# Four of eight pairs by seven products in the two feed-forwards, five and six of twenty-two in the first one's second product, and TensorE's order tied to the source

## The chip, the cores and the metric

The kernel runs on one core of a Trainium2 chip. The metric is the device time of one execution in microseconds. A core has five engines with a queue each, which run side by side and wait for one another by semaphores: TensorE (PE, matrix products; its weight loads, PEld, overlap the products), VectorE (DVE), ScalarE (ACT), GpSimd (POOL) and SyncE (SP). DMA transfers are issued from the queues of SP, ScalarE and GpSimd, and run on 16 DMA engines.

## The reference

One encoder layer on 256 tokens of width 2048, everything in float32: a feed-forward, a token mixer, a cross-attention into 256 memory tokens, and a second feed-forward, each behind an RMS norm and added to its input, with a last norm at the end. The change touches the two feed-forwards (hidden width 5632):

```python
def swiglu_ffn(h, w_in, w_out):
    gate, up = jnp.split(h @ w_in, 2, axis=-1)
    return (jax.nn.silu(gate) * up) @ w_out

h = rms_norm(x, ffn1_norm[l])
x = x + MACARON_SCALE * swiglu_ffn(h, ffn1_w_in[l], ffn1_w_out[l])
...
h = rms_norm(x, ffn2_norm[l])
x = x + MACARON_SCALE * swiglu_ffn(h, ffn2_w_in[l], ffn2_w_out[l])
```

## The kernel before, in words

**Products in parts.** Both sides of a float32 product are split into a high part (a cast to the type fp32r) and a low part, the remainder, and three matmuls are summed for a product: high by high, high by low, low by high (`three`, L316 to 320, and `by_two`, L322 to 334). A weight tile has 128 rows (one k) and 1024 columns. `raw` (L403 to 409) issues its load from SP into one of several raw buffers, and `parts` (L392 to 401) splits it: ScalarE casts the high part (L397), VectorE subtracts for the remainder (L398). The split buffers are used in rotation: three called hl, two called ring, and in the first feed-forward one called more from its second group on.

**Groups.** The first product of a feed-forward (by `w_in`) runs over 11 groups (`NG`) of 512 hidden features, 512 gate and 512 up columns, so a weight tile is 128x1024. A group has 16 tiles, taken as 8 pairs of neighbours. Group 0 is plain. In groups 1 to 10 (`group`, L527) the letters of a pattern (L37) say how each pair is done:

- C (`eight`, L492): two plain tiles, 12 matmuls of 128x128 by 128x512 each, into the four banks "2", "3", "4", "8".
- S (`seven`, L464): the pair is seen as a product of 2x2 blocks and done with seven block products in place of eight, as in Winograd's form of Strassen's method, so 21 matmuls in place of 24. Its seven products go into banks "5", "7", "6", "1", "2", "3", "4". It needs four split weight tiles, and I call them by their names in the code: the sums (1024 wide, formed by VectorE at L470 and 471 from the two raw tiles), "one" (1024; its left half updated at L477), "two" (1024, as loaded) and a half tile (512; "two" updated at L484). The sums serve products 5 and 7, "one" serves 6 and 1, "two" serves 2 and 3, the half tile serves 4. The four matching forms of x are made once, by `sides` (L435), beside group 0.

After the last S pair of a group `joins_sevens` (L520) puts its own four banks together: a copy of bank "1" by ScalarE (L521) and four VectorE adds (L522 to 525), which read the four `spare` slices p1, u2, u4, u5. After the last pair come the end adds (L550), one each for the banks "2", "4", "3", "8", and `give` (L507): two silus on ScalarE (L510), two multiplies on VectorE (L512). The buffer `spare` also holds the sums, some of the raw tiles and the raw tiles of the summed ones.

**Summed tiles.** A few plain tiles of a group, listed in `SUMMED` (L39), are not split by VectorE. `summed` (L419) loads them from SP (L425), ScalarE writes the negated high part (L426) and then the high part (L427), and a DMA that accumulates, issued from GpSimd (L428), adds the raw tile to the negated part. They have two buffers, hl_s and, in the first feed-forward, half of more. In the second feed-forward, groups 8 to 10 have one such buffer and the list `ALONE` (L40).

**The second product.** In the first feed-forward, the second product (by `w_out`, 44 tiles of 128x1024 for each of two output blocks in use here, that is 22 pairs a block) is done by `out_block` (L553) with the same `seven` and `eight`; `OUT_S` (L44) lists the S pairs and `OUT_STEPS` (L45) the order. Their x-side forms come out of `out_sides` (L580), behind the transposes of the hidden features (`turning`, L300, and `turn`, L656). The second product of the second feed-forward is done by `gemm_n` (L192) and not touched.

**What orders the work.** The program is built through a tile scheduler that simulates the engines' timelines and sets the order of each engine's queue from that. Work that the source lists later can so come earlier in a queue, matmuls of different pairs too. `tc.issue_after(ins)` adds an edge: what is issued inside it on the engine of `ins` stands behind `ins` in that engine's queue.

Of the kernel before, what the change touches and what calls it, by code (L numbers as in the profile page):

```python
# [11 lines left out]
F32 = mybir.dt.float32  # L12
# [32 lines left out]
OUT_STEPS = (  # L45
    [0, 1, 2, 3, 4, 5, 6, 7, 8, 10, 11, 9, 13, 14, 12, 16, 17, 15, 18, 19, 20, 21],
    [9, 0, 1, 12, 2, 3, 15, 4, 5, 18, 6, 7, 8, 10, 11, 13, 14, 16, 17, 19, 20, 21],
# [31 lines left out]
def layer(ctx: ExitStack, tc: tile.TileContext, a: dict):  # L79
# [220 lines left out]
    def turning(o, c, sink):  # L300

        def go():
            tp = pa.tile([P, 2, T], F32, name="aux")
            for k in range(2):
                for t in range(2):
                    nc.tensor.transpose(  # L306
                        out=tp[:, k, t * P:(t + 1) * P], in_=o[:, t, c + k * P:c + (k + 1) * P], identity=ident
                    )
            sink(tp)
        return go  # L310
# [5 lines left out]
    def three(acc, x, hi, lo, first, last):  # L316
# [3 lines left out]
        nc.tensor.matmul(acc, lhsT=x[1], rhs=hi, start=False, stop=last)  # L320

    def by_two(acc, x, hi, lo, k, first, last):  # L322
# [5 lines left out]
        for t in range(2):  # L328
# [4 lines left out]
            for g in range(2):  # L333
                nc.tensor.matmul(acc[t][g], lhsT=x[:, 1, s], rhs=hi[:, cols[g]], start=False, stop=last)  # L334
# [7 lines left out]
    class FeedForward:  # L342
# [6 lines left out]
        def __init__(self, stack, tags, x_hl, gain, w_in, pattern, summed, w_out=None, pair=False):  # L349
# [34 lines left out]
            self.next = None  # L384
# [34 lines left out]
        def summed(self, at):  # L419
# [5 lines left out]
            nc.sync.dma_start(out=raw, in_=self.w_in[j, :, k])  # L425
# [32 lines left out]

        def begins(self, name):
# [4 lines left out]
        def seven(self, j, p, b, last):  # L464

            k = 2 * p
# [19 lines left out]
            three(b["4"], self.half(j, k + 1, 1), w[:, 0, lo], w[:, 1, lo], self.begins("4"), False)  # L486
# [5 lines left out]
        def eight(self, j, p, b, last, plain, between=None):  # L492
            for k in (2 * p, 2 * p + 1):
# [7 lines left out]
                by_two(acc, self.x(j, k), w[:, 0], w[:, 1], k, begin, last and k % 2 == 1)  # L501
# [18 lines left out]
        def joins_sevens(self, b, p1, u2, u4, u5):  # L520
# [4 lines left out]
            nc.vector.tensor_tensor(out=u5, in0=u2, in1=b["5"], op=ALU.add)  # L525

        def group(self, j, r, after=()):  # L527
# [8 lines left out]
            n = len(self.pattern)  # L536
            for p, c in enumerate(self.pattern):
                if c == "S":
                    self.seven(j, p, b, p == self.spairs[-1])
                    if p == self.spairs[-1]:  # L540
                        self.joins_sevens(b, p1, u2, u4, u5)
                else:
                    late = p > self.spairs[-1] and len(after) > 0
                    self.eight(j, p, b, p == n - 1, late)
                    if p > self.spairs[-1] + 1:
# [110 lines left out]
        def turn(self, i):  # L656

            def go():
# [17 lines left out]
                turning(self.h[i // 2], i % 2 * 2 * P, both)()  # L676
# [13 lines left out]
    with ExitStack() as stack:  # L690
# [7 lines left out]
        def x_more(k):  # L698
# [4 lines left out]
            if k in (6, 9, 12):  # L703
                ff.sides(k // 3 - 2)
# [665 lines left out]
```

## Time and profile before

| what | value |
|---|---|
| three runs | 2089.42, 2089.99, 2090.06 us |
| their median | 2089.99 us |
| the profiled execution | 2088.91 us, its span 2087.1 us |
| mean granted TensorE clock | 0.999 |
| TensorE busy | 2076.4 us, 99% |
| VectorE busy | 1622.5 us, 78% |
| ScalarE busy | 1174.4 us, 56% |
| GpSimd busy | 66.0 us, 3% |

The span goes from the first to the last instruction; the time of the execution holds 1.8 us more. In the lines of the profile, each row names a line of the code, the engine, the operation, what is written and read, the shape, and then, by the view, counts, busy time and the mean of one. PE, PEld, DVE, ACT, POOL and SP are the engines; a name with q behind it is an engine's queue where it issues DMAs. A timeline's row begins with the start in microseconds from the span's start and the time until the last one of the row is through; `x3` at its end says that three instructions stand together, and brackets hold the idle time before the row and what ended it. A window's row has the stretch, its length, the busy time and the number of instructions of PE, PEld, DVE, ACT and POOL, the granted TensorE clock, the DMA engines' busy share and GB/s. Instruction times are those of one execution.

### The profile page before, as it was taken

The page shows a single profiled execution, that of the slowest core. Times are in us where ns is not written, and L with a number is a line of the kernel's source. Part 1 is how long each engine was busy: PE and PEld are TensorE (multiplying, and loading weights), DVE is VectorE, ACT ScalarE, POOL GpSimd, SP SyncE. Part 2 cuts the span into 40 slices and gives each one's busy share as a digit, 9 for nine tenths or more (in the row PEclk, how much of TensorE's full clock was granted, in tenths as well). Part 3 has the DMA queues.
Part 4 walks back from the last instruction along what each step waited for, and adds up shares of the span by engine and source line. Part 5 has one row for each costly group of instructions (what it writes and reads, how often), then busy time and mean ns, then how long its engine had stood idle before and what let it go on. Part 6 is the DMA issues. An engine that isn't in the chain of part 4 may idle for free.

```text
span 2087.1 us, 26730 instructions
## 1 busy us (share of the span) xinstructions
PE 2076.4 (99%) x9765; PEld 1739.0 (83%) x9765; DVE 1622.5 (78%) x2302; ACT 1174.4 (56%) x1470; POOL 66.0 (3%) x81
## 2 busy tenths in 40 slices
PE   9999999999999999999999999999999999999998
PEld 8888888888888888888888899888888888888886
DVE  7888888877777689989877666778888888787754
ACT  8665666555545554445764455566665655554443
POOL 0000000000000000000000000000000000000000
PEclk9999999999999999999999999999999999999999
DMA  9787778755566576655555543687777777556664
GB/s 366 246 263 246 232 223 263 230 182 192 188 203 234 180 238 199 186 179 187 180 196 192 184 160 124 200 291 224 237 236 253 222 217 230 169 166 203 195 192 152
DMA packets 122245, 441.30 MB, mean 211 GB/s; under 512 B 13569, under 2 KB 13953, under 8 KB 121729
## 3 DMA queue, kind: packets, MB, share of 16 engines
q1 hardware_dynamic: 113184, 407.08, 57.1%
q0 software_dynamic: 8352, 31.46, 8.1%
q8 instruction: 76, 1.25, 0.2%
q10 hardware_dynamic: 576, 1.06, 0.1%
q14 instruction: 57, 0.46, 0.1%
HBM read 437.44 MB, written 2.10 MB: 211 GB/s over the span
## 4 chain that ended last, share of the span: by engine, by line
PE 87%; issue 11%; POOL 1%; DMA 1%; ACT 0%; DVE 0%; DVEq 0%; POOLq 0%
PE acc L332 11%; PE acc L331 11%; PE acc L334 11%; PE acc L204 8%; PE acc L205 8%; PE acc L203 8%; PE acc L154 8%; PE acc L162 4%; PE acc L318 3%; PE acc L319 3%; PE acc L320 3%; PE aux L306 1%; PE aux L318 1%; PE aux L319 1%; PE aux L320 1%
## 5 line engine op out<-in xcount | busy, mean ns | idle before, releaser
L124 ACT CAST hl<-raw 128x1024 fp32r<-128x1024 f32 (+1 forms) x315 | 327.1, 1040 | 358.9 <-PE acc L205 191.9
L125 DVE TENSOR_TENSOR hl<-raw,hl 128x1024 fp32r<-128x1024 f32 (+1 forms) x315 | 381.2, 1212 | 165.0 <-ACT hl L124 163.6
L397 ACT CAST hl<-raw 128x1024 fp32r<-128x1024 f32 (+1 forms) x151 | 147.6, 988 | 117.3 <-PE acc L334 48.2
L398 DVE TENSOR_TENSOR hl<-raw,hl 128x1024 fp32r<-128x1024 f32 (+1 forms) x151 | 172.2, 1145 | 47.4 <-ACT hl L397 45.7
L398 DVE TENSOR_TENSOR hl<-spare,hl 128x1024 fp32r<-128x1024 f32 (+1 forms) x125 | 144.7, 1162 | 32.5 <-ACT hl L397 30.3
L397 ACT CAST hl<-spare 128x1024 fp32r<-128x1024 f32 (+1 forms) x125 | 124.3, 1002 | 66.4 <-PE acc L334 24.2
L332 PE MATMUL acc<-hl,x_hl 128*128 128x512 f32 x388 | 140.9, 390 | 0.1
L331 PE MATMUL acc<-hl,x_hl 128*128 128x512 f32 x388 | 135.7, 390 | 0.0
L334 PE MATMUL acc<-hl,x_hl 128*128 128x512 f32 x388 | 120.6, 390 | 0.0
L397 ACT CAST ring<-spare 128x1024 fp32r<-128x1024 f32 (+1 forms) x83 | 82.1, 993 | 59.6 <-issue 19.1
L398 DVE TENSOR_TENSOR ring<-spare,ring 128x1024 fp32r<-128x1024 f32 (+1 forms) x83 | 95.2, 1150 | 20.3 <-ACT ring L397 19.6
L332 PE MATMUL acc<-ring,x_hl 128*128 128x512 f32 x276 | 101.3, 389 | 0.0
L204 PE MATMUL acc<-hl,x_hl 128*128 128x512 f32 x256 | 100.7, 393 | 0.0
L204 PE MATMUL acc<-hl,m_hl 128*128 128x512 f32 x256 | 100.4, 392 | 0.0
L205 PE MATMUL acc<-hl,m_hl 128*128 128x512 f32 x256 | 100.3, 392 | 0.0
L205 PE MATMUL acc<-hl,x_hl 128*128 128x512 f32 x256 | 100.0, 391 | 0.0
L331 PE MATMUL acc<-ring,x_hl 128*128 128x512 f32 x276 | 98.6, 390 | 0.0
L203 PE MATMUL acc<-hl,m_hl 128*128 128x512 f32 x256 | 90.9, 392 | 0.0
L203 PE MATMUL acc<-hl,x_hl 128*128 128x512 f32 x256 | 90.2, 392 | 0.0
L334 PE MATMUL acc<-ring,x_hl 128*128 128x512 f32 x276 | 86.2, 389 | 0.0
L332 PEld LDWEIGHTS acc<-hl,x_hl 128*128 128x128 f32 x388 | 72.6, 188 | 15.5 <-DVE hl L133 0.4
L334 PEld LDWEIGHTS acc<-hl,x_hl 128*128 128x128 f32 x388 | 72.9, 188 | 15.1
(518 smaller groups left out, 5100.8 us busy)
## 6 DMA issues: line engine op xcount, KB each, us to landing
spare<-in_ffn_w_in SPq DMA_DIRECT2D x184, 512.0 KB, 6.8
raw<-in_ffn_w_in SPq DMA_DIRECT2D x157, 512.0 KB, 5.9
raw<-in_ffn_w_out SPq DMA_DIRECT2D x138, 512.0 KB, 4.0
hl_s<-in_ffn_w_in POOLq DMA_DIRECT2D x42, 512.0 KB, 8.3
raw<-in_w_mix_vg SPq DMA_DIRECT2D x32, 512.0 KB, 4.3
raw<-in_w_k SPq DMA_DIRECT2D x32, 512.0 KB, 3.6
raw<-in_w_v SPq DMA_DIRECT2D x32, 512.0 KB, 4.0
raw<-in_w_mix_out SPq DMA_DIRECT2D x32, 512.0 KB, 4.4
```

The source lines that it names most:

```text
L124: nc.scalar.copy(out=hl[:, 0, :size], in_=raw[:, :size])
L125: newest[0] = nc.vector.tensor_tensor(out=hl[:, 1, :size], in0=raw[:, :size], in1=hl[:, 0, :size].bitcast(F32), op=ALU.subtract)
L154: done = nc.tensor.matmul(acc, lhsT=hi[:, k], rhs=xs[k], start=first and k == 0, stop=last and k == kk - 1, skip_group_check=True,)
L162: done = nc.tensor.matmul(acc[:, 0], lhsT=lo[:, k], rhs=xs[k][:, 0], start=False, stop=last and k == kk - 1, skip_group_check=True,)
L203: nc.tensor.matmul(acc[t], lhsT=x[:, 0, s], rhs=hi[:, k], start=k0 + k == 0, stop=False)
L204: nc.tensor.matmul(acc[t], lhsT=x[:, 0, s], rhs=lo[:, k], start=False, stop=False)
L205: nc.tensor.matmul(acc[t], lhsT=x[:, 1, s], rhs=hi[:, k], start=False, stop=k0 + k == nk - 1)
L331: nc.tensor.matmul(acc[t][g], lhsT=x[:, 0, s], rhs=hi[:, cols[g]], start=(t, g) in first, stop=False)
L332: nc.tensor.matmul(acc[t][g], lhsT=x[:, 0, s], rhs=lo[:, cols[g]], start=False, stop=False)
L334: nc.tensor.matmul(acc[t][g], lhsT=x[:, 1, s], rhs=hi[:, cols[g]], start=False, stop=last)
L397: self.cast = nc.scalar.copy(out=hl[:, 0, :n], in_=raw[:, :n])
L398: newest[0] = nc.vector.tensor_tensor(out=hl[:, 1, :n], in0=raw[:, :n], in1=hl[:, 0, :n].bitcast(F32), op=ALU.subtract)
```

## The change

The pattern of a group has four S pairs in place of three, at pairs 0, 2, 4, 6, and so the last S pair is the last but one. Group 10 of both feed-forwards and groups 8 to 10 of the second keep the old pattern (`FEWER`), so 9 groups of the first and 7 of the second change. The summed tiles are k = 2, 6, 10, 14 in place of 2, 7, 13. The second product of the first feed-forward has 5 and 6 S pairs in its two blocks in place of 3 and 4, with S and C alternating in the first block from the step at which they begin, and in the second from its start; the buffers are parted otherwise for the two more forms. The summed tiles' raw loads are issued by GpSimd.

Two kinds of ties are new. `tied` holds TensorE's order to the source: each S pair, each plain tile and each pair of transposes is issued behind the last matmul of the one before. And an S pair's VectorE work (the sums, updates and remainders of `seven`) is issued behind `joined`, the last of the four joins of the group (or block) before.

The core of the diff (with the longer tables left out):

```diff
-PATTERNS = ("SCSCSCCC", "SCSCSCCC")
-SUMMED = ((2, 7, 13), (2, 7, 13))
+PATTERNS = ("SCSCSCSC", "SCSCSCSC")
+FEWER = "SCSCSCCC"
+SUMMED = ((2, 6, 10, 14), (2, 6, 10, 14))
+SIDES = (4, 7, 10, 13)
-OUT_S = ((9, 12, 15), (9, 12, 15, 18))
+OUT_S = ((9, 11, 13, 15, 17), (9, 11, 13, 15, 17, 19))
...
             j, k = self.sums_at[at]
-            nc.sync.dma_start(out=raw, in_=self.w_in[j, :, k])
+            nc.gpsimd.dma_start(out=raw, in_=self.w_in[j, :, k])
...
+        def tied(self):
+            return nullcontext() if self.pe is None else tc.issue_after(self.pe.ins)
...
         def seven(self, j, p, b, last):
+            with self.tied(), nullcontext() if self.joined is None else tc.issue_after(self.joined.ins):
+                self.seven_products(j, p, b, last)
+
+        def seven_products(self, j, p, b, last):
             k = 2 * p
...
-            three(b["4"], self.half(j, k + 1, 1), w[:, 0, lo], w[:, 1, lo], self.begins("4"), False)
+            self.pe = three(b["4"], self.half(j, k + 1, 1), w[:, 0, lo], w[:, 1, lo], self.begins("4"), False)
...
-                by_two(acc, self.x(j, k), w[:, 0], w[:, 1], k, begin, last and k % 2 == 1)
+                with self.tied():
+                    self.pe = by_two(acc, self.x(j, k), w[:, 0], w[:, 1], k, begin, last and k % 2 == 1)
...
-            nc.vector.tensor_tensor(out=u5, in0=u2, in1=b["5"], op=ALU.add)
+            self.joined = nc.vector.tensor_tensor(out=u5, in0=u2, in1=b["5"], op=ALU.add)
...
-            n = len(self.pattern)
-            for p, c in enumerate(self.pattern):
+            pattern = FEWER if j == NG - 1 or self.pair and j > 7 else self.pattern
+            n, done = len(pattern), pattern.rindex("S")
+            for p, c in enumerate(pattern):
...
-            self.sums_at = [(j, k) for j in range(1, NG) for k in sums if j < NG - 1 or k < min(14, sums[-1])]
+            self.sums_at = [(j, k) for j in range(1, NG) for k in sums if j < NG - 1 or k < 13]
...
-                turning(self.h[i // 2], i % 2 * 2 * P, both)()
+                with self.tied():
+                    self.pe = turning(self.h[i // 2], i % 2 * 2 * P, both)()
...
-                ff.ring += [more[:, q] for q in range(2)]
-                forms = more[:, 2:].rearrange("p a two n -> p (a two n)")
+                ff.ring.append(more[:, 0])
+                forms = more[:, 1:].rearrange("p a two n -> p (a two n)")
...
-                rest["raws"] = [pool.tile([P, 1024], F32, name=f"raw_out{q}") for q in range(2)]
+                ff.ring.append(pool.tile([P, 2, 1024], F32R, name="hl_out"))
...
-        ff.raws = rest["raws"]
-        xT = xt.tile([P, KD, T], F32, name="xT", tag="x")
-        for k in range(0, KD, 8):
-            nc.gpsimd.dma_start(out=xT[:, k:k + 8], in_=a["xT"][:, k:k + 8])
...
         def beside_second(i):
             if i == OUT_STEPS[1].index(OUT_S[1][-1]):
-                ff.ring = []
+                ff.raws, ff.ring = [], ff.ring[1:]
+                xT = xt.tile([P, KD, T], F32, name="xT", tag="x")
...
-            elif i > 9:
+            elif i > 10:
                 beside(1.4)
-                if i % 2 == 0 and turns:
+                if i > 12 and i % 2 == 0 and turns:
...
-            if k in (6, 9, 12):
-                ff.sides(k // 3 - 2)
+            if k in SIDES:
+                ff.sides(SIDES.index(k))
```

VectorE at the boundary from group 5 to group 6 of the first feed-forward, in the program before. L398 are remainders; by their targets and by what stands around them, ring<-spare (first) is that of the next pair's sums, ring<-spare (second) that of "one", more<-spare that of "two", and hl<-spare of 512 that of the half tile, all of group 6's first pair; L484 updates "two" for that half tile. L470, 471 and 477 belong to its second S pair. L524 and L525 are the last two joins of group 5, L550 its first end add.

```order
L398 TENSOR_TENSOR ring_131<-spare_132,ring_131 128x1024
L524 TENSOR_TENSOR spare_132<-spare_132,aux_1680 128x512
L398 TENSOR_TENSOR ring_131<-spare_132,ring_131 128x1024
L470 TENSOR_TENSOR spare_132<-raw_2052 128x512
L471 TENSOR_TENSOR spare_132<-raw_2054,raw_2052 128x512
L525 TENSOR_TENSOR spare_132<-spare_132,acc_1679 128x512
L398 TENSOR_TENSOR more_490<-spare_132,more_490 128x1024
L477 TENSOR_TENSOR raw_2052<-spare_132,raw_2054 128x512
L484 TENSOR_TENSOR spare_132<-spare_132 128x512
L398 TENSOR_TENSOR hl_2014<-spare_132,hl_2014 128x512
L550 TENSOR_TENSOR spare_132<-spare_132,acc_1683 128x512
```

The whole first pair of group 6 stands ahead of group 5's first end add, and the sums of it ahead of the third join. In the program after, the same engine from the last join (L541) on; here L485 and 486 form the sums of group 6's first pair, ring<-raw is the remainder of "two" (raw_2021), L492 the update of "one", L567 the four end adds, L499 the update of "two", hl<-spare the remainder of the sums, hl<-raw that of tile 3 (a plain tile of pair 1) and ring<-spare that of "one".

```order
L541 TENSOR_TENSOR spare_132<-spare_132,acc_1709 128x512
L485 TENSOR_TENSOR spare_132<-spare_132 128x512
L486 TENSOR_TENSOR spare_132<-raw_2021,spare_132 128x512
L404 TENSOR_TENSOR ring_131<-raw_2021,ring_131 128x1024
L492 TENSOR_TENSOR spare_132<-spare_132,raw_2021 128x512
L567 TENSOR_TENSOR spare_132<-spare_132,acc_1713 128x512
L567 TENSOR_TENSOR spare_132<-spare_132,acc_1714 128x512
L499 TENSOR_TENSOR raw_2021<-raw_2021,spare_132 128x512
L567 TENSOR_TENSOR spare_132<-spare_132,acc_1715 128x512
L404 TENSOR_TENSOR hl_2025<-spare_132,hl_2025 128x1024
L567 TENSOR_TENSOR spare_132<-spare_132,acc_1716 128x512
L404 TENSOR_TENSOR hl_2071<-raw_2069,hl_2071 128x1024
```

All of the pair's work now stands behind the last join and lies mixed with the end adds; the remainder of "one" comes behind the last of them, and that of the half tile is further back. ScalarE at the same boundary before: L521 is the joins' copy, L397 are casts (ring twice: the sums and "one"; more: "two"; hl of 512: the half tile; the last one: tile 3), L426 and 427 the negated copy and the cast of a summed tile.

```order
L521 COPY spare_132<-acc_1682 128x512
L397 CAST hl_1932<-raw_1930 128x1024
L397 CAST hl_1953<-raw_1951 128x1024
L397 CAST ring_131<-spare_132 128x1024 x2
L397 CAST more_490<-spare_132 128x1024
L397 CAST hl_2014<-spare_132 128x512
L426 ACTIVATE hl_s_133<-spare_132 128x1024
L427 CAST hl_s_133<-spare_132 128x1024
L397 CAST hl_2033<-spare_132 128x1024
```

The casts of the pair stand ahead of the summed tile's negated copy. After, L537 is the joins' copy, ring<-raw_2021 the cast of "two", L432 and 433 the negated copy and the cast of a summed tile into the buffer that tile k = 14 leaves, hl<-spare the cast of the sums, hl<-raw that of tile 3, ring<-spare that of "one", L526 a silu.

```order
L537 COPY spare_132<-acc_1712 128x512
L403 CAST ring_131<-raw_2021 128x1024
L432 ACTIVATE more_498<-spare_132 128x1024
L433 CAST more_498<-spare_132 128x1024
L403 CAST hl_2025<-spare_132 128x1024
L403 CAST hl_2071<-raw_2069 128x1024
L403 CAST ring_131<-spare_132 128x1024
L526 ACTIVATE h5_125<-spare_132,r_x2_109 128x512
```

The casts of the sums and of "one" now stand behind the negated copy, and "two" alone ahead of it. In both programs TensorE's matmuls of the pair follow behind group 5's last tile; after, in the source's order.

More of the change, by code (lines that the diff above doesn't have):

```diff
@@ L1 @@
 from collections import deque
[L2 removed]
+from contextlib import ExitStack, nullcontext
 import numpy as np
@@ L309, in go @@
             sink(tp)
+            return done
         return go
@@ L319, in three @@
         nc.tensor.matmul(acc, lhsT=x[0], rhs=lo, start=False, stop=False)
-        nc.tensor.matmul(acc, lhsT=x[1], rhs=hi, start=False, stop=last)
+        return nc.tensor.matmul(acc, lhsT=x[1], rhs=hi, start=False, stop=last)
     def by_two(acc, x, hi, lo, k, first, last):
@@ L333, in by_two @@
             for g in range(2):
-                nc.tensor.matmul(acc[t][g], lhsT=x[:, 1, s], rhs=hi[:, cols[g]], start=False, stop=last)
+                done = nc.tensor.matmul(acc[t][g], lhsT=x[:, 1, s], rhs=hi[:, cols[g]], start=False, stop=last)
+        return done
     def bank(pool, name):
```

26 lines of the change are left out of this document (14 added, 12 removed).

## The prediction

> **What bounds the kernel now.** I read the page first, then the list of waits of TensorE, then windows of one group's length, and last the timelines of three engines around one group boundary. The page and the list of waits:
>
> ```profile
> span 2087.1 us, 26730 instructions
> PE 2076.4 (99%) x9765; PEld 1739.0 (83%) x9765; DVE 1622.5 (78%) x2302; ACT 1174.4 (56%) x1470; POOL 66.0 (3%) x81
> PE aux L232 <- DVE ones L229: 1.1, 1, 1.1
> PE acc L332 <- DMA hl_s<-in_ffn_w_in: 0.8, 1, 0.8
> ```
>
> TensorE is busy for 99% of the span and waits 1.9 us in all. So the kernel lasts as long as its matmuls take at the rate at which TensorE issues them, and no other engine costs anything as long as it keeps TensorE fed. What I need of an average group is the issue rate and the room of the others (columns: PE, PEld, DVE, ACT, POOL busy with instructions, granted clock, DMA share, GB/s):
>
> ```profile
> 213.90:255.38 41.48, 41.48 (x184) 34.36 (x184) 34.41 (x41) 26.03 (x29) 2.60 (x3) 1.00 0.78 243
> ```
>
> This is one group. Its code has 3 pairs of 21 matmuls and 5 of 24, that is 183 (the cut counts one more), so a matmul goes out every 41.48 / 183 = 0.2267 us. VectorE has 7.1 us to spare in it, ScalarE 15.4 us.
>
> Now the boundary between two groups, as it stands before (into group 8, first feed-forward). TensorE starts the next group at 339.75; I call that moment E, and times below are relative to it.
>
> ```profile
> 333.63 0.39 PE L332 MATMUL acc<-hl_s,x_hl 128*128 128x512 f32 x1
> ...
> 337.94 0.62 PE L334 MATMUL acc<-ring,x_hl 128*128 128x512 f32 x2
> ...
> 339.30 0.62 PE L334 MATMUL acc<-ring,x_hl 128*128 128x512 f32 x2
> 339.75 0.39 PE L318 MATMUL acc<-more,ring 128*128 128x512 f32 x1
> ```
>
> ```profile
> 319.84 1.03 ACT L427 CAST more<-spare 128x1024 fp32r<-128x1024 f32 x1
> 320.78 1.04 ACT L397 CAST hl<-spare 128x1024 fp32r<-128x1024 f32 x1
> 321.72 0.58 ACT L521 COPY spare<-acc 128x512 f32<-128x512 f32 x1
> ...
> 334.06 1.06 ACT L426 ACTIVATE hl_s<-spare 128x1024 fp32r<-128x1024 f32 x1 [2.85 <-PE acc L332]
> 335.03 1.04 ACT L427 CAST hl_s<-spare 128x1024 fp32r<-128x1024 f32 x1
> 336.23 0.62 ACT L397 CAST hl<-raw 128x512 fp32r<-128x512 f32 x1 [0.17 <-DVE raw L484]
> ...
> 342.32 0.72 ACT L510 ACTIVATE h<-spare,r_x 128x512 f32<-128x512 f32 x1
> 343.00 1.05 ACT L397 CAST hl<-spare 128x1024 fp32r<-128x1024 f32 x1
> ```
>
> ```profile
> 338.37 0.69 DVE L550 TENSOR_TENSOR spare<-spare,acc 128x512 f32<-128x512 f32 x1 [0.79 <-PE acc L334]
> 338.97 1.22 DVE L398 TENSOR_TENSOR ring<-spare,ring 128x1024 fp32r<-128x1024 f32 x1
> 340.11 1.88 DVE L550 TENSOR_TENSOR spare<-spare,acc 128x512 f32<-128x512 f32 x3
> 341.90 0.75 DVE L512 SCALAR_TENSOR_TENSOR h<-spare,r_x,h 128x512 f32<-128x512 f32 x1
> 342.56 1.22 DVE L398 TENSOR_TENSOR ring<-spare,ring 128x1024 fp32r<-128x1024 f32 x1
> ```
>
> Three things are to be seen. First, the prices in a full queue, start to start: VectorE 0.60 us for 128x512, 1.14 for 128x1024, 0.66 for a give; its results are there 0.69, 1.22 and 0.75 after the start. ScalarE 0.97 for the negated copy of a summed tile, 0.94 for a 1024-wide cast (done after 1.05), 0.48 for the join's copy (done after 0.58), 0.68 for a silu, 0.62 until a 512-wide cast is done. Second, both queues stop for TensorE: ScalarE's negated copy starts at 334.06, 0.04 us after the matmul of 333.63 is through (0.39 long), and VectorE idles 0.79 us before the first end add. Third, this costs nothing here, because all four weight tiles of the next group's first pair stand ahead of the end adds in VectorE's queue, and ahead of that negated copy or just behind it in ScalarE's.
>
> **The change, part by part.** The gain is plain. Of 16 groups one pair more goes from 24 to 21 matmuls, and 4 pairs more of the 44: 20 x 3 = 60 matmuls, which the built programs confirm (9726 before, 9666 after). 60 x 0.2267 = 13.6 us, if TensorE stays fed.
>
> VectorE's load can still be carried. A group gains 8 of its operations (5 x 0.60 + 3 x 1.14 = 6.4 us) and loses three remainders (3.4 us), since now four of eight ordinary tiles are summed ones: 34.4 + 3.0 = 37.4 us of 40.8. Inside a group, S and C pairs alternate: 10.2 us of TensorE against 6.4 + 1.1 us of VectorE. I followed the queues through one group of each kind and found every weight tile ready before its product. In the second product (S with two plain tiles, 8.7 us of VectorE in 10.2) each remainder also stands ahead of whatever waits for TensorE. I cost all this at nothing; the cover is five or more split buffers, two pairs of work.
>
> At the group's end the cover is gone. Two edits do it. The last S pair is now pair 6, not pair 4, so the joins can start only one C pair before the end; and the next group's S pair is tied behind the last join, so none of its VectorE work can go earlier. On top, the summed tile k = 14 lies in that last C pair, and ScalarE's negated copy into its buffer waits for it.
>
> Take the boundary into group 6, whose queues are shown with the change. Slots of 0.2267 us run back from E: pair 6 takes slots -45 to -25, tile 14 -24 to -13, tile 15 -12 to -1. ScalarE: the copy of product 1 waits for slot -34 (through at -7.32) and is done at -6.70. The negated copy waits for tile 14's tenth matmul (slot -15, through at -3.01) and starts at -2.97, its cast at -2.00, then the cast of the sums at -1.06 (done -0.01), of tile 3 at -0.12, of "one" at 0.82 (done 1.87), a silu at 1.76, the half cast at 2.44 (done 3.06). VectorE: joins at -6.66, -6.06, -5.46, -4.86; sums at -4.26 and -3.66; remainder of "two" -3.06; update of "one" -1.92; the first end add, whose gate (slot -8) opened at -1.42, at -1.32; the next at -0.72, update of "two" -0.12, third end add 0.48, remainder of the sums 1.08 (done 2.30), fourth end add 2.22, tile 3 at 2.82, remainder of "one" 3.96 (done 5.18), give 5.10, half remainder 5.76 (done 6.45).
>
> TensorE, in its own order: first products of 5 and 7 at 0.03 and 0.26; those of 6 and 1 wait for the cast of "one" and go at 1.91; all of 2 and 3 follow at 2.37 and 3.05, the first of 4 at 3.73, the rest of 5 and 7 at 3.95; the rest of 6 and 1 waits for its remainder until 5.22, the rest of 4 until 6.49. The pair ends at 6.95 instead of 21 x 0.2267 = 4.76: 2.2 us lost.
>
> There are five kinds of boundary; each is worked the same way from its queues. Into groups 3, 6, 9 of the first feed-forward: 2.2. Into 4, 7, 10 tile 3 stands behind the pair, "one" is cast at -0.12 and its remainder done at 4.04, the half remainder at 5.31: the pair ends at 5.80, 1.0 lost. Into 2, 5, 8 the update of "two" comes last of all: remainder of the sums 0.59, "one" 2.33, "two" 3.47, then two sums of the following pair and two gives, the update at 7.13, the half cast done at 8.48, one more update and remainder, the half remainder at 9.47 (done 10.16). TensorE waits from 5.6 to 8.5 and from 8.8 to 10.2 and ends at 10.65: 5.9 lost. Into 2 to 7 of the last feed-forward: half remainder done at 6.45 as above, 2.2 each; into 8, where no negated copy stands in the way but two sums do, 3.4. The shortened groups behind have the old order, 0. Sum: 3 x (2.2 + 1.0 + 5.9) + 6 x 2.2 + 3.4 = 27.3 + 16.6 = 43.9 us.
>
> The trace of before has no such stall, so I bound it. The nearest row from below is the 0.8 us in the list of waits; from above, a VectorE that does nothing of the pair ahead of time, 6.4 us of its work. What I take lies between, at the queue's own prices. Elsewhere: loads for summed tiles move from SP to POOL, ahead of the accumulating DMA.
>
> ```profile
> hl_s<-in_ffn_w_in POOLq DMA_DIRECT2D x42, 512.0 KB, 8.3
> 0.74 0.86 SPq L603 DMA_DIRECT2D raw<-in_ffn_w_in  x2
> 5.37 0.47 PE L331 MATMUL acc<-hl,x_hl 128*128 128x512 f32 x1
> 3.20:4.50 1.30, 1.30 (x8) 1.30 (x8) 0.00 (x0) 0.58 (x2) 0.00 (x0) 1.00 1.07 383
> ```
>
> An accumulation lands 8.3 us after its issue and has over 15 us until its tile is used, so it stays hidden. SP loses a queue's worth of waits that cost nothing. But POOL's first load now waits for nothing and goes out beside the first weights, with the DMA engines full: 524 KB at 383 GB/s is 1.4 us ahead of the first matmul, or nothing if it comes second. I take 0.7.
>
> Sum against the profiled execution (2088.91): -13.6 + 43.9 + 0.7 = +31.0, 2119.9. The median of the three runs is 1.1 us higher, so 2121 us.
>
> **Rivals.** (1) The queues run ahead as before and the matmuls saved are all that counts: 2089.99 - 13.6 + 0.7 = 2077 us, faster. For it: VectorE keeps 3 us to spare per group, and the trace has no wait at any boundary. Against: the order after. It decides at a stall of 13.6 / 16 = 0.85 us per boundary. 5%.
>
> (2) Only ScalarE's gate counts, VectorE being earlier than I think: 1.5, 0.5, 1.0 and 0.5 us by kind, 12 us in all, 2089 us: the same. 3%.
>
> (3) TensorE slows down after the long stalls. The rows that bear on it:
>
> ```profile
> 1.10:3.20 2.10, 2.10 (x10) 2.10 (x11) 0.00 (x0) 1.49 (x3) 0.21 (x1) 1.00 0.62 160
> 717.94 0.93 PE L306 MATMUL aux<-ident,o 128*128 128x128 f32 x7
> 2075.00:2087.00 12.00, 3.35 (x15) 2.44 (x13) 5.05 (x14) 4.31 (x10) 2.56 (x2) 0.86 0.45 175
> ```
>
> Coming from idle, the first 128-wide matmuls stand 0.21 us apart, those at 718 us (0.93 - 0.27) / 6 = 0.11; and the granted clock falls to 0.86 in the tail, where TensorE has run dry. If a stall of the longest kind (one matmul between 5.6 and 10.2) did the same, the 21 or so matmuls behind it would take 4.8 us more, in three places: +14 us, 2135. Against it: shorter idle times leave the clock at 1.00. 13%. [...]
>
> (4) The accumulating DMAs come late, now that two DMAs a tile share POOL's queue and DMA is at 0.82: at 2 us a group, 32 us more, 2153. Against: 15 us of cover. 7%.
>
> **The numbers.** The forecast has 72%. Its own errors are the stall's prices, 30% low (2107) to 15% high (2128). The range 2106 to 2142 takes in rival 3 and leaves out rivals 1, 2 and 4, 15%. A measurement here tells 0.2% (4 us) from no change: faster 0.05, same 0.03, slower 0.92.
>
> **What would show it.** In the profile after, the groups should show 180 matmuls in some 42 to 47 us instead of 41.5; TensorE's list of waits should name ScalarE's casts and VectorE's remainders of the split tiles with about 44 us, all at group ends, none in the second product. If waits are under 15 us, I am wrong; if they lie inside the groups, the mechanism is another; if the clock falls below 1.00 at the boundaries, it is rival 3.

## The result and the profile after

The changed kernel takes 2144.66 us (median of four runs, 2143.42 to 2145.36) against 2090.02 us: slower, ratio 1.0263, 95% interval 1.025 to 1.0275. That is 54.6 us more, where the forecast was 31 and its range ended at 2142. The profiled execution took 2145.36 us, 56.4 more than the one of before.

The page after, its span and the engines' busy time, and the largest entries of TensorE's list of waits:

```profile
span 2143.6 us, 26789 instructions
PE 2096.7 (98%) x9705; PEld 1728.2 (81%) x9705; DVE 1691.4 (79%) x2427; ACT 1221.3 (57%) x1539; POOL 121.2 (6%) x171
...
PE acc L324 <- DVE ring L404: 13.2, 12, 2.4
PE acc L323 <- ACT ring L403: 7.8, 3, 2.6
PE acc L324 <- DVE more_out L404: 2.2, 1, 2.2
```

TensorE has 60 matmuls fewer and yet 20 us more busy time: 13.6 us of work went, so some 34 us of "busy" came in without a matmul more. In the rows below matmuls stand 0.427 us apart at a granted clock of 0.50, in place of 0.2267, and single ones beside a wait count 0.39 and 0.49 us of busy time. The waits are the ones the prediction named (L324 waits for a remainder, L323 for a cast), and there is an entry in the second product (more_out) that it did not. The prediction looked for about 44 us in this list, all at group ends; the entries for casts, remainders and end adds in the groups add up to some 32, those of the second product to 3.0, and the rest of the loss stands in TensorE's busy time.

Four groups, each from its first matmul to the next group's first (columns as in the windows before). The first three are groups 5, 6 and 7 of the first feed-forward, the last is group 4 of the second one. A group now has 180 matmuls, 180 x 0.2267 = 40.8 us:

```profile
227.44:277.09 49.65, 45.17 (x181) 35.20 (x180) 37.47 (x47) 28.00 (x32) 5.70 (x8) 0.93 0.73 210
277.09:321.06 43.97, 42.18 (x182) 33.40 (x181) 37.10 (x47) 27.95 (x32) 5.67 (x8) 1.00 0.81 239
321.06:363.40 42.34, 41.82 (x182) 33.48 (x181) 36.86 (x47) 27.80 (x32) 5.70 (x8) 1.00 0.86 251
1537.23:1580.73 43.50, 42.09 (x182) 33.41 (x181) 37.21 (x47) 28.04 (x32) 5.69 (x8) 1.00 0.81 242
```

They lose 8.8, 3.2, 1.5 and 2.7 us, where the hand-made queues gave 5.9, 2.2, 1.0 and 2.2: the kinds of boundary are right, the period of three too. Nearly all of it lies in the first two pairs of the group; groups 3, 6 and 9 lose 0.4 to 0.5 us more in their third S pair. VectorE's 36.9 to 37.5 us a group are as forecast (37.4). The first row alone has a granted clock below 1.00.

Inside that row, TensorE around the longest wait, and four windows of 3.41 us from it on:

```profile
233.19 0.39 PE L325 MATMUL acc<-hl,ring 128*128 128x512 f32 x1
236.17 0.49 PE L323 MATMUL acc<-ring,x_hl 128*128 128x512 f32 x1 [2.59 <-ACT ring L403]
237.86 0.80 PE L324 MATMUL acc<-ring,x_hl 128*128 128x512 f32 x1 [1.20 <-DVE ring L404]
238.45 0.63 PE L325 MATMUL acc<-ring,x_hl 128*128 128x512 f32 x1
238.88 0.63 PE L336 MATMUL acc<-hl_s,x_hl 128*128 128x512 f32 x1
```

```profile
233.13:236.54 3.41, 0.82 (x3) 0.20 (x2) 3.41 (x6) 1.97 (x3) 0.00 (x0) 1.00 0.03 5
236.54:239.95 3.41, 2.21 (x6) 1.71 (x6) 3.41 (x5) 2.52 (x3) 0.00 (x0) 0.50 0.76 243
239.95:243.37 3.42, 3.42 (x9) 2.65 (x9) 3.42 (x5) 0.21 (x1) 0.00 (x0) 0.50 0.15 60
243.37:246.78 3.41, 3.41 (x16) 2.79 (x16) 0.94 (x2) 2.64 (x4) 1.39 (x2) 1.00 0.94 252
```

The pair's last product waits twice, 2.59 and 1.20 us, with one matmul between, and then the matmuls go out every 0.427 us in place of 0.2267 until 243.4. The granted clock is 0.50 for 6.83 us, from 236.54 to 243.37. VectorE meanwhile is busy without a gap (3.41 of 3.41 us in the first window). What it does first:

```profile
232.25 0.68 DVE L485 TENSOR_TENSOR spare<-spare 128x512 f32<-128x512 f32 x1
232.86 0.74 DVE L528 SCALAR_TENSOR_TENSOR h<-spare,r_x,h 128x512 f32<-128x512 f32 x1
233.52 0.68 DVE L486 TENSOR_TENSOR spare<-spare 128x512 f32<-128x512 f32 x1
234.12 0.74 DVE L528 SCALAR_TENSOR_TENSOR h<-spare,r_x,h 128x512 f32<-128x512 f32 x1
234.78 0.68 DVE L499 TENSOR_TENSOR raw<-raw 128x512 f32<-128x512 f32 x1
235.38 0.68 DVE L492 TENSOR_TENSOR spare<-spare 128x512 f32<-128x512 f32 x1
235.99 1.22 DVE L404 TENSOR_TENSOR more<-spare,more 128x1024 fp32r<-128x1024 f32 x1
237.12 0.68 DVE L404 TENSOR_TENSOR ring<-raw,ring 128x512 fp32r<-128x512 f32 x1
```

The update that the half tile needs (L499) stands behind two sums of the following pair and two gives; its remainder (the last row) behind one update and one remainder more of that following pair. None of these six is needed yet.

The second product, which the prediction costed at nothing, has the same picture once, in its first S pair:

```profile
571.50 0.50 PE L323 MATMUL acc<-more_out,hA 128*128 128x512 f32 x1 [0.80 <-ACT more_out L403]
574.20 0.59 PE L324 MATMUL acc<-more_out,hA 128*128 128x512 f32 x1 [2.20 <-DVE more_out L404]
```

The windows of that pair with the next one (45 matmuls, 10.2 us), and of group 8 of the last feed-forward (183 matmuls, 41.5 us):

```profile
566.46:581.83 15.37, 12.37 (x47) 9.51 (x45) 12.96 (x17) 6.28 (x7) 0.00 (x0) 0.89 0.44 154
1754.70:1801.46 46.76, 43.46 (x185) 35.23 (x183) 40.87 (x50) 26.52 (x30) 2.84 (x4) 0.96 0.68 209
```

5.2 and 5.3 us are lost, with granted clocks of 0.89 and 0.96. The start costs too: group 0 takes 45.98 us, before 44.02.

### The profile page after: what moved, and what is told of

Same layout as the page of the kernel before. It is cut to its first block, busy times and chain, and to the rows that moved or that the text cites. A ratio compares the mean times of both kernels' runs of the same rounds, so it can differ in the third digit from the quotient of the medians.

```text
span 2143.6 us, 26789 instructions
## 1 busy us (share of the span) xinstructions
PE 2096.7 (98%) x9705; PEld 1728.2 (81%) x9705; DVE 1691.4 (79%) x2427; ACT 1221.3 (57%) x1539; POOL 121.2 (6%) x171
## 3 DMA queue, kind: packets, MB, share of 16 engines
q8 instruction: 76, 1.25, 0.2%
## 4 chain that ended last, share of the span: by engine, by line
PE 82%; DVE 12%; issue 2%; DMA 2%; ACT 1%; POOL 0%; SPq 0%; DVEq 0%; ACTq 0%
PE acc L337 9%; PE acc L336 9%; PE acc L339 9%; PE acc L158 8%; PE acc L208 8%; PE acc L209 8%; PE acc L207 8%; PE acc L166 4%; PE acc L324 3%; PE acc L325 3%; PE acc L323 3%; DVE hl L404 2%; DVE spare L567 2%; DVE ring L404 1%; PE aux L323 1%
## 5 line engine op out<-in xcount | busy, mean ns | idle before, releaser
L129 DVE TENSOR_TENSOR hl<-raw,hl 128x1024 fp32r<-128x1024 f32 (+1 forms) x315 | 380.7, 1210 | 162.6 <-ACT hl L128 161.1
L404 DVE TENSOR_TENSOR hl<-raw,hl 128x1024 fp32r<-128x1024 f32 (+1 forms) x143 | 165.4, 1161 | 49.0 <-ACT hl L403 47.4
L404 DVE TENSOR_TENSOR hl<-spare,hl 128x1024 fp32r<-128x1024 f32 (+1 forms) x141 | 165.7, 1182 | 33.1 <-ACT hl L403 31.7
L403 ACT CAST hl<-spare 128x1024 fp32r<-128x1024 f32 (+1 forms) x141 | 142.3, 1019 | 78.0 <-DVE spare L486 35.3
L337 PE MATMUL acc<-hl,x_hl 128*128 128x512 f32 x372 | 135.9, 390 | 0.3 <-DVE hl L137 0.2
L336 PE MATMUL acc<-hl,x_hl 128*128 128x512 f32 x372 | 131.3, 391 | 0.5 <-ACT hl L403 0.5
L339 PE MATMUL acc<-hl,x_hl 128*128 128x512 f32 x372 | 114.9, 389 | 0.0
L404 DVE TENSOR_TENSOR ring<-spare,ring 128x1024 fp32r<-128x1024 f32 (+1 forms) x81 | 86.9, 1075 | 21.9 <-ACT ring L403 21.4
L208 PE MATMUL acc<-hl,x_hl 128*128 128x512 f32 x256 | 100.8, 394 | 0.4 <-DVE hl L129 0.3
L209 PE MATMUL acc<-hl,x_hl 128*128 128x512 f32 x256 | 100.0, 391 | 0.0
L403 ACT CAST ring<-spare 128x1024 fp32r<-128x1024 f32 (+1 forms) x81 | 75.3, 932 | 33.8 <-PE acc L325 15.1
L404 DVE TENSOR_TENSOR ring<-raw,ring 128x512 fp32r<-128x512 f32 (+1 forms) x74 | 77.2, 1046 | 18.6 <-ACT ring L403 18.1
L207 PE MATMUL acc<-hl,x_hl 128*128 128x512 f32 x256 | 90.9, 392 | 0.0
L403 ACT CAST ring<-raw 128x512 fp32r<-128x512 f32 (+1 forms) x74 | 67.0, 909 | 36.1 <-PE acc L325 16.3
L336 PE MATMUL acc<-hl_s,x_hl 128*128 128x512 f32 x216 | 87.3, 404 | 0.0
L337 PE MATMUL acc<-hl_s,x_hl 128*128 128x512 f32 x216 | 87.2, 404 | 0.0
L434 POOL DMA_DIRECT2D hl_s<-in_ffn_w_in x54 | 47.2, 873 | 633.3 <-ACT hl_s L432 633.3
```

The source lines that it names most:

```text
L129: newest[0] = nc.vector.tensor_tensor(out=hl[:, 1, :size], in0=raw[:, :size], in1=hl[:, 0, :size].bitcast(F32), op=ALU.subtract)
L207: nc.tensor.matmul(acc[t], lhsT=x[:, 0, s], rhs=hi[:, k], start=k0 + k == 0, stop=False)
L208: nc.tensor.matmul(acc[t], lhsT=x[:, 0, s], rhs=lo[:, k], start=False, stop=False)
L209: nc.tensor.matmul(acc[t], lhsT=x[:, 1, s], rhs=hi[:, k], start=False, stop=k0 + k == nk - 1)
L336: nc.tensor.matmul(acc[t][g], lhsT=x[:, 0, s], rhs=hi[:, cols[g]], start=(t, g) in first, stop=False)
L337: nc.tensor.matmul(acc[t][g], lhsT=x[:, 0, s], rhs=lo[:, cols[g]], start=False, stop=False)
```

## The experiments

Theory 1: the order of VectorE's queue at a group's end makes the waits, and the tie behind the last join sets that order. Theory 2: with four S pairs, the last one next to the end, VectorE (or ScalarE) has too much to do there in any order. Theory 3: the tied order of TensorE costs the time. The medians, each beside the kernel before on the same chip (2089.62 to 2089.64 us):

| run | us | ratio, 95% interval |
|---|---|---|
| e1 no join tie | 2118.20 | 1.0138 (1.0123 to 1.0153) |
| e2 no join tie, end adds behind joins | 2103.39 | 1.0068 (1.0053 to 1.0083) |
| e3 old pattern, all ties | 2087.75 | 0.9992 (0.9982 to 1.0001) |
| e4 longest wait filled | 2139.67 | 1.0243 (1.0226 to 1.026) |
| e5 tie behind the half tile | 2085.18 | 0.998 (0.9971 to 0.999) |
| e6 as e5, end adds behind joins | 2082.02 | 0.9965 (0.9952 to 0.9978) |
| e7 three summed tiles | 2169.63 | 1.0384 (1.0368 to 1.0399) |
| e8 summed loads from SP | 2143.21 | 1.0255 (1.0238 to 1.0272) |
| e9 as e6, loads from SP | 2081.95 | 0.9961 (0.9948 to 0.9975) |
| e10 no tie on TensorE | 2137.92 | 1.0233 (1.0219 to 1.0247) |
| e11 both waits filled | 2137.26 | 1.0229 (1.0215 to 1.0243) |

### Taking the tie out (e1, e2)

```diff
-            with self.tied(), nullcontext() if self.joined is None else tc.issue_after(self.joined.ins):
+            with self.tied():
```

> The tie of an S pair's VectorE work behind the last join is taken out, all else as in the changed kernel. Theory 1 (the tie puts the next group's first pair behind joins and end adds): the long waits at the group ends go. The order now has the last join between or behind the first end adds, and the first product of the next group needs the bank that this join frees, so 0.6 us is left at each of 9 boundaries and 1.2 at each of 7: 14 us in place of the 63 measured, 2095 us (2090 to 2101), granted clock 1.00 at all boundaries. Theory 2 (with four S pairs and the last one at pair 6, VectorE and ScalarE are too full at a group's end, whatever the tie): the waits stay, over 2130 us. Theory 3 (the tied order of TensorE costs the time): no change, 2144 us.

2118.20 us: the tie was worth 26 us of the 54.6, not nearly all. The list of waits of e1 says what came in its place:

```profile
PE acc L323 <- DVE spare L567: 20.5, 13, 3.3
PE aux L323 <- DVE spare L540: 4.2, 3, 1.7
```

In the groups TensorE no longer waits for weights but for banks. Now the pair's work runs ahead and the joins and end adds (L567) late, and product 4 of the next group needs the bank that an end add frees. e2 adds the tie of the end adds:

```diff
-                nc.vector.tensor_tensor(out=u, in0=u, in1=b[acc], op=ALU.add)
+                with tc.issue_after(self.joined.ins):
+                    nc.vector.tensor_tensor(out=u, in0=u, in1=b[acc], op=ALU.add)
```

> As e1, and the end adds are tied behind the last join instead, so that the join comes early and the pair's work stays ahead of it. Theory 1: no wait of over 0.5 us at a boundary; what is left over the matmuls saved (13.6 us) is the start (2 us) and the second product's first S pair (5 us): 2084 us (2079 to 2089), faster than before. Theory 2: over 2130 us. Theory 3: about 2144 us.

2103.39 us. 15 us better than e1, 19 worse than expected. TensorE still waits 5.5 us for a join (L540) and 5.5 us for remainders of the groups' tiles (L404). The numbers of both runs lay between theory 1 and theory 2; they did not decide it.

### The old pattern with the new ties (e3)

```diff
-PATTERNS = ("SCSCSCSC", "SCSCSCSC")
+PATTERNS = ("SCSCSCCC", "SCSCSCCC")
-SIDES = (4, 7, 10, 13)
+SIDES = (4, 7, 10)
```

> The pattern of a group goes back to three S pairs with the last at pair 4 (SCSCSCCC, 183 matmuls a group), with both ties, the four summed tiles, the loads from GpSimd and the changed second product kept. Theory 1 (tie and late last pair together make the wait): the joins come two pairs earlier, so no wait at a group's end: 2090 - 2.7 (12 matmuls of the second product) + 5 (its first S pair) + 2 (start) = 2094 us (2091 to 2099). Theory 3 (the tied order of TensorE costs the time by itself): over 2110 us. Theory 2 says 2094 as well.

2087.75 us: with the old pattern, whose last S pair lies two pairs further from the end, neither tie costs anything. The waits over 0.8 us are two, 1.1 at the start and 0.9 in front of a transpose. It came out below the 2094 expected because the second product's first S pair has no wait here: the order was rearranged there too, and the half tile's remainder stands behind the next pair's sums, but ahead of its update and its remainders. So theory 3 fails, and the tie hurts only together with the new pattern. Whether there by its order (theory 1) or by its load (theory 2), e3 does not say: both expected 2094.

### Another tie (e5, e6)

```diff
             w = self.parts(two, G)
+            self.joined = newest[0]
...
-            self.joined = nc.vector.tensor_tensor(out=u5, in0=u2, in1=b["5"], op=ALU.add)
+            nc.vector.tensor_tensor(out=u5, in0=u2, in1=b["5"], op=ALU.add)
```

> The tie of an S pair's VectorE work is moved: it stands behind the half tile's remainder of the S pair before, not behind the last join. So the pairs keep their order among themselves and the next group's first pair may go ahead of joins and end adds, and no later pair's sums can get ahead of a half tile. Theory 1 (the order of VectorE's queue makes the waits): 2090 - 13.6 for the matmuls, + 2 at the start, + 1 in the second product's first S pair, + up to 0.6 at 16 boundaries, because the last join still stands behind two end adds: 2085 us (2080 to 2092), granted clock 1.00 throughout. Theory 2 (VectorE is too full at a group's end: joins 2.4, end adds 2.4, gives 1.3 and the pair's 6.4 us are 12.5 us in the 10.2 us of the last C and the first S pair): no better than the 2103 of e2, 2103 to 2118 us.

> As e5, and the end adds are tied behind the last join as in e2. Theory 1: the 0.6 us at the boundaries goes as well, 2081 us (2078 to 2086). Theory 2: 2103 us or more, as e2.

e6 keeps a handle on the last join and ties the end adds behind it, as e2 does. 2085.18 and 2082.02 us: both as theory 1 had them, and both below the kernel before, by 0.2% and 0.35%, with intervals that leave out 1. One group of e6, from group 4's first matmul to group 5's, and VectorE at the boundary that ends it:

```profile
174.36:215.16 40.80, 40.80 (x181) 33.80 (x180) 37.24 (x46) 28.11 (x32) 5.72 (x8) 1.00 0.86 255
```

```profile
213.46 0.68 DVE L541 TENSOR_TENSOR spare<-spare,aux 128x512 f32<-128x512 f32 x1
214.06 0.68 DVE L499 TENSOR_TENSOR raw<-raw 128x512 f32<-128x512 f32 x1
214.66 0.68 DVE L542 TENSOR_TENSOR spare<-spare,acc 128x512 f32<-128x512 f32 x1
215.26 2.47 DVE L569 TENSOR_TENSOR spare<-spare,acc 128x512 f32<-128x512 f32 x4
217.65 0.68 DVE L404 TENSOR_TENSOR ring<-raw,ring 128x512 fp32r<-128x512 f32 x1
218.25 0.68 DVE L485 TENSOR_TENSOR spare<-spare 128x512 f32<-128x512 f32 x1
```

The same 37.2 us of VectorE, the same four S pairs, and not one wait in this group: 180 matmuls in 40.80 us. Of the next group's first pair only the half tile is still open here: its update (L499) stands between the last two joins (L541, L542), its remainder (512 wide) behind the four end adds, and the following pair's sums (L485) only then. This boundary leads into group 5, one of the three worst of the changed kernel. Theory 2 fails: the load fits.

### ScalarE's gate (e7)

```diff
-SUMMED = ((2, 6, 10, 14), (2, 6, 10, 14))
+SUMMED = ((2, 6, 10), (2, 6, 10))
```

> Of the four summed tiles k = 14 is made plain: ScalarE has no negated copy that waits for the last C pair, and VectorE one remainder more a group (1.14 us, 38.5 of 40.8). The tie of the changed kernel stays. If ScalarE's gate sets the long waits, as the prediction's hand-made queues have it (casts of the sums and of 'one' behind it), the pair's half remainder is done 6.5 us after the group's start at every boundary, 2.2 us lost each, no wait long enough for the clock: 16 x 2.2 = 35 in place of 63, 2118 us. If VectorE's load sets them, the added remainder makes it worse: 16 x 1.1 = 18 us more, 2162 us.

2169.63 us, 25 more than the changed kernel. TensorE's list has 16.7 + 10.7 + 7.9 us of waits for remainders (L404) and 5.9 + 4.8 for casts. Without the negated copy of tile 14 the boundaries became worse, so taking that gate away does not cure the waits, and most of what is waited for is VectorE's. How much of the 25 us is the added remainder and how much the order, which was rearranged as well, the run does not separate.

### The loads (e8, e9)

```diff
-            nc.gpsimd.dma_start(out=raw, in_=self.w_in[j, :, k])
+            nc.sync.dma_start(out=raw, in_=self.w_in[j, :, k])
```

> The summed tiles' raw loads go back to SP's queue. The first one then no longer runs beside the first weights: the second weight tile lands 1.1 us earlier, 2143.5 us (2142 to 2144). If GpSimd's queue had cost anything else in the groups (an accumulating DMA issued late), up to 30 us less; if SP's queue holds weight loads up behind the summed ones, more than 2145.

> The ties of e6 and the summed tiles' loads from SP as in e8. If the two costs are independent: 2082.0 - 1.4 (e8 against the changed kernel) = 2080.6 us, first group 44.2 us long as in e8. If SP's queue is what the reordered kernel lives on, more than 2082.

e8: 2143.21 us; group 0 takes 44.16 us there, as before. The loads from GpSimd cost the start 1.8 us. In the groups they cost nothing that shows: no DMA stands in the changed kernel's list of waits. In e9 group 0 is shorter than in e6 too (44.2 against 45.8 us), but the whole is not: 2081.95 against 2082.02. The 1.4 us are below what these runs resolve.

### TensorE's order, and its clock (e10, e4, e11)

e10 takes out the other tie (`tied` does nothing).

> Only the tie of TensorE's order is taken out of the changed kernel; the S pairs' VectorE work stays tied behind the last join. The order now puts up to 24 matmuls of the next C pair (its summed tile is ready) ahead of the products that wait. If TensorE loses its time because its own order is fixed: the long waits of groups 2, 5 and 8 and their half rate go (3 x 8.7 us) and most of the others (13 x 1.5), 2099 us. If VectorE's order is the cause and filling only puts the wait off to the next product that needs VectorE, the time stays above 2130 us.

2137.92 us: 6.7 us of 54.6. Its list of waits has 12.6 us for a cast at product 6 or 7 where the long waits of the changed kernel are filled, and 4.3 us for summed tiles whose accumulation is late. Filling puts most of the wait off to the next product.

e4 and e11 add matmuls that nothing needs into the wait of the three worst groups (e4 in short; e11 with 13, and 6 more into bank "8" behind product 4's first matmul):

```diff
+            if p == 0 and j in (2, 5, 8) and not self.pair:
+                with tc.issue_after(third.ins):
+                    for _ in range(10):
+                        nc.tensor.matmul(b["4"], lhsT=form[3][0], rhs=full[:, 0, hi], start=True, stop=True)
```

> Ten matmuls whose result is overwritten are put into TensorE's longest wait, ahead of product 4 of the first pair of groups 2, 5 and 8 of the first feed-forward; nothing else is changed and nothing waits for them but product 4 (10 x 0.227 = 2.3 us of a wait of 3.0). If the half rate behind that wait (0.427 us a matmul for some 12 matmuls, granted clock 0.50) comes from TensorE standing idle, these three places run at 0.227 again: 3 x 2.9 = 8.7 us less than the changed kernel, 2136 us. If it comes from something else (the queues or the DMAs of that moment), the time stays at 2144 us or grows by up to 7 us.

> As e4, with 13 filling matmuls in the first wait and 6 more, into a bank not yet begun, in the second one between product 4's first and second matmul (1.7 us). All filling results are overwritten. If idleness is what halves the rate, none of the three places is slow any more: 3 x 2.9 = 8.7 us less than the changed kernel, 2136 us. If one of them is still slow, idleness is not the whole cause.

2139.67 and 2137.26 us: 5.0 and 7.4 less than the changed kernel, by doing more. In e4, groups 2 and 8 ran at the full rate behind the wait, and group 5 had still eight matmuls at some 0.43. In e11, group 5 as the others (compare the row 227.44 to 277.09 of the changed kernel, and its matmuls from 238.45 on):

```profile
226.45:273.58 47.13, 46.41 (x200) 36.95 (x199) 37.58 (x47) 27.94 (x32) 5.69 (x8) 1.00 0.76 222
```

```profile
232.44 3.12 PE L505 MATMUL acc<-hl,ring 128*128 128x512 f32 x13
235.40 0.40 PE L509 MATMUL acc<-ring,x_hl 128*128 128x512 f32 x1
235.64 1.55 PE L512 MATMUL acc<-hl,ring 128*128 128x512 f32 x6
237.03 0.39 PE L514 MATMUL acc<-ring,x_hl 128*128 128x512 f32 x1
237.26 0.39 PE L515 MATMUL acc<-ring,x_hl 128*128 128x512 f32 x1
```

The clock stays at 1.00 and the matmuls behind the wait are 0.23 apart. So in these three places the half rate came from TensorE standing idle. From the changed kernel's trace to this one groups 2, 5 and 8 get shorter by 1.9, 2.5 and 2.8 us: the half rate cost 7.2 us in these three places, 2.4 each. What is left of the wait there is 47.13 - 40.80 = 6.3 us, against 5.9 in the prediction.

## Why the prediction was too low, step by step

**The gain** was right: 60 matmuls, 13.6 us. e6 shows a group at 40.80 us, and keeps 7.6 of the 13.6 over all; what it lacks is spread over the start, short waits and one wait ahead of a transpose (0.9 us).

**"VectorE's load can still be carried"** was right, 36.9 to 37.5 us a group measured, and e6 shows it.

**The stalls at the group ends.** The mechanism was right, named by its cause (first pair behind the joins, mixed with the end adds), and e5 and e6 show it. In a sum by boundaries:

| place | predicted | measured |
|---|---|---|
| groups 2, 5, 8 of the first feed-forward | 17.7 | 26.2 |
| groups 3, 6, 9 | 6.6 | 9.4 |
| groups 4, 7, 10 | 3.0 | 4.6 |
| groups 2 to 7 of the last one | 13.2 | 16.1 |
| its group 8 | 3.4 | 5.3 |
| second product | 0 | 5.2 |
| start | 0.7 | 2.0 |
| matmuls | -13.6 | -13.6 |
| sum | 31.0 | 55.2 |

(The 1.2 us to the measured 56.4 lie in the stage between the feed-forwards, which is 1.2 us longer and which the change does not touch. Two small waits outside the table cancel: one of 0.9 us in front of a transpose is new, and the 0.8 us for a summed tile that the kernel before had in the last feed-forward are gone.)

Four terms were mis-sized. First, **the clock**, and this is the step that failed. The sum lets TensorE go on at the full rate behind every stall; the half rate was left to rival 3, put at 13% with the reason that "shorter idle times leave the clock at 1.00". It happened, in all three places named and in two more. It cost 7.2 us in the three (e11), 2.4 each, where the rival had 4.8. The other two are the granted clocks of 0.96 and 0.89 above, 3.41 us at half rate each; that makes, as an estimate, some 1.5 and 1.7 us lost. Without the half rate in these three places the time would be some 2137 us, inside the range. The range held this rival alone (2135), but not together with the terms below.

Second, **the second product**: "each remainder also stands ahead of whatever waits for TensorE" is true of the pairs that were looked at in the steady run, and false for its first S pair, where the half tile's remainder stands behind the next pair's sums, its update of "one" and two of its remainders, much as in groups 2, 5 and 8. With the half tile's tie (e5) this pair loses 1.25 us in place of 5.2.

Third, **the prices inside a stall**, some 0.45 us at each boundary. Group 6's first pair in the changed kernel: VectorE at the four joins and the first sum, TensorE at the pair's last two matmuls and the next one.

```profile
270.40 0.69 DVE L538 TENSOR_TENSOR spare<-spare,aux 128x512 f32<-128x512 f32 x1 [4.79 <-ACT spare L537]
271.12 0.69 DVE L539 TENSOR_TENSOR spare<-spare,acc 128x512 f32<-128x512 f32 x1
271.84 0.69 DVE L540 TENSOR_TENSOR spare<-spare,aux 128x512 f32<-128x512 f32 x1
272.56 0.69 DVE L541 TENSOR_TENSOR spare<-spare,acc 128x512 f32<-128x512 f32 x1
273.17 0.68 DVE L485 TENSOR_TENSOR spare<-spare 128x512 f32<-128x512 f32 x1
```

```profile
283.91 0.50 PE L324 MATMUL acc<-more,x_hl 128*128 128x512 f32 x1
284.25 0.39 PE L325 MATMUL acc<-more,x_hl 128*128 128x512 f32 x1
284.48 0.40 PE L336 MATMUL acc<-hl_s,x_hl 128*128 128x512 f32 x1
```

The joins begin where the hand-made queue had them (6.69 us before the group's first matmul at 277.09, by hand 6.66), but they go 0.72 us apart in place of 0.60. Every VectorE instruction behind them is in the forecast order and some 0.33 us later than forecast: the remainder of "one" at 4.29 in place of 3.96, that of the half tile at 6.09 in place of 5.76. No run tests why joins in a row take longer; they work on the same few slices. The other 0.11 us is TensorE's: the matmul behind one that had to wait comes 0.34 us later (283.91 to 284.25), not 0.2267. Together 2.2 became 2.6, and the other kinds show it too. The 0.4 to 0.5 us that groups 3, 6 and 9 lose in their third S pair stand in no term of the prediction.

Fourth, **the start**: 1.96 us, not 0.7. With GpSimd's load beside the first weights the second weight tile's cast began at 7.97 us in place of 6.87; 0.9 us more go at 34 us. e8 gives nearly all of it back.

**ScalarE's gate**, which the prediction named as a second cause "on top", is there, but nothing shows that it costs time. In group 6 the negated copy starts at 274.09 after 2.77 us of idling for tile 14, the cast of "one" follows at 277.89, and product 6 waits 1.15 us for it, as forecast. But the pair ends with VectorE's remainders, and VectorE works from 270.40 to 285 without a gap, so an earlier cast would not end it sooner. e7, which takes the gate away, made the waits longer.

Of the other rivals, 1 (no stalls, 2077 us) is what another order nearly reaches (2082). Against 2 (VectorE earlier than thought) speaks its queue, 0.33 us later than forecast. Against 4 (accumulating DMAs late) speaks the list of waits after, in which no DMA stands.

## What to carry to other kernels

An engine with 9% to spare (VectorE in e6: 37.24 us of 40.80) can still stop the one that it feeds: look at the order of its queue where two stages meet, and ask of each tie what now stands behind the tied instruction, and which of it is needed first. A tie that keeps work of one kind in its own sequence (pair behind pair, join ahead of end add) was worth 62 us here over a tie that puts the next stage's first step behind the last stage's end. When waits of 2 to 3 us are forecast on TensorE, price slower matmuls behind them as well: behind the waits of 2.59 and 1.20 us in group 5 they stood 0.427 us apart in place of 0.2267 and cost some 2.4 us; behind e1's wait of 2.72 us they stood 0.23 apart. Count the waits that lie close together: in e4, with the first filled, 0.32 and 1.19 us were left in group 5 and eight matmuls still went at some 0.43.

## What the runs showed of the hardware

TensorE's rate halved at some waits of 2 to 3 us, and the length of one wait does not decide it. In e1 two boundaries have waits of the same length:

```profile
145.31 0.77 PE L323 MATMUL acc<-more,x_hl 128*128 128x512 f32 x1 [2.71 <-DVE spare L567]
```

```profile
275.74 0.47 PE L323 MATMUL acc<-more,x_hl 128*128 128x512 f32 x1 [2.72 <-DVE spare L567]
```

Behind the first the matmuls go out every 0.43 us, behind the second every 0.23. The granted clock around them, in stretches of 3.41 us, the first wait above and the second below:

```profile
141.56:144.97 3.41, 1.04 (x5) 0.50 (x3) 3.41 (x6) 1.10 (x2) 0.00 (x0) 1.00 1.02 347
144.97:148.38 3.41, 3.07 (x7) 2.49 (x8) 3.41 (x6) 1.77 (x2) 0.00 (x0) 0.50 0.46 183
```

```profile
271.27:274.68 3.41, 1.75 (x8) 1.05 (x6) 3.41 (x6) 1.81 (x2) 0.00 (x0) 1.00 1.03 297
274.68:278.09 3.41, 2.35 (x10) 1.99 (x11) 3.41 (x6) 1.78 (x2) 0.00 (x0) 1.00 0.68 278
```

At the first wait the clock is 0.50 from 144.97 to 148.38, at the second it stays at 1.00. The first wait lies nearly whole in the 3.41 us ahead of 144.97, in which TensorE is busy for 1.04 us; the two stretches around the second share its wait and hold 1.75 and 2.35 us. Such a figure goes with where the stretch is cut: the 3.41 us up to the end of the second wait, at 275.74, hold at most 3.41 - 2.72 = 0.69 us, and the clock did not fall there. So neither the length of the wait nor the busy time just ahead of its end tells the two apart, and no run here tests what does.

In the changed kernel the clock falls to 0.50 five times between start and tail, each time within a wait of 2.20 to 2.59 us or less than 1 us behind one:

| where | clock falls at, us | stays at 0.50 for, us | TensorE busy in the 3.41 us before, us |
|---|---|---|---|
| group 2 | 100.01 | 6.83 | 1.67 |
| group 5 | 236.54 | 6.83 | 0.82 |
| group 8 | 373.07 | 6.83 | 0.49 |
| second product | 574.46 | 3.41 | 0.76 |
| group 8 of the last feed-forward | 1762.30 | 3.41 | 1.19 |

The first three falls lie 136.53 us apart; three groups of this kernel last 136.0 us (227.44 to 363.40).
